# A hybrid decoder layer on one NeuronCore: preparing two RWKV head pairs together, and taking x from a transposed copy

## The chip, the cores and the metric

The kernel runs on one core of a Trainium2 chip. A core has TensorE (PE in the profile; its weight loads are PEld), VectorE (DVE), ScalarE (ACT), GpSimd (POOL) and SyncE (SP), which only issues transfers here. Matmul results go to PSUM, everything else lies in SBUF. The metric is the device time in microseconds of one execution, the median of several runs.

## The reference: what is computed

One layer over 2048 tokens of width 1024, in float32. With h = RMSNorm(x), one projection p = h @ w_in gives the inputs of three branches, their gates, and three merge gates:

```
y_a = rwkv7_mix(p_r, p_k, p_v, p_w, p_a, ...) * silu(z_a)        # 8 heads of 64, delta rule
y_b = sliding_window_sink_attn(p_q, p_sk, p_sv, ...) * silu(z_b)  # window 128
y_c = memory_cross_attn(p_xq, mem, ...) * silu(z_c)               # 256 memory tokens
merged = sum over i of sigmoid(gate_i) * (y_i @ w_proj_i)
out = x + merged @ w_out
```

The part that the change touches most is the RWKV branch. Per head, with a state S, it computes at each token

```
kk = k * k_k / max(norm(k * k_k), 1e-12)        # norm over the 64 channels of a head
k  = k * (1 + (a - 1) * k_a)
S  = S * w + (S @ -kk) (kk * a)^T + v k^T ;  y = S @ r
bonus = sum(r * k * r_k) * v                     # sum over the 64 channels
```

and then normalizes y per head and adds the bonus.

## The kernel before, in words

The tokens are worked in four blocks of 512 (`TB`). For block 0 the weights come from their inputs, are split into a high and a low part (L403 and L404) and kept in DRAM; the later blocks load the split form. A float32 product is made of three matmuls of the dense kind (L421 to L423 in `gemm3`; L1077 to L1079 in the output): high by high, high by low, low by high. Other products and all transposes run on plain float32 operands.

h is kept channels by tokens. `x_norm` loads 128x512 pieces of x with tokens on rows, squares and sums them, scales the rows (L450), and transposes them on TensorE (L455), and L459 and L460 split the result into `hH` and `hL`.

In a block two streams are woven: `stream_r`, the RWKV branch, and `stream_f`, the cross-attention heads, the sliding-window heads, the merges of those two branches and the gates of the third. After both follow the merge of the RWKV branch, `x_norm` for the next block, and `output`.

`stream_r` takes the eight heads as four pairs (128 rows hold two heads) and two pairs as a group. For each pair `rwkv_prep` projects k, computes decay and rates, and takes the key norm: squares, a matmul with `bones` that sums over a head's channels (L471, tokens on rows), a reciprocal, and `bcast_T`, which spreads the eight columns over channels (L480) and transposes them back (L482) so that L675 can scale by them. Gram matrices of the 8 chunks of 64 tokens follow (L701, masked at L706 and L707), and then the inverse of a unit triangular matrix per chunk: within 32x32 blocks by substitution on VectorE, 31 steps of a shuffle and two tensor operations (L720 to L722), and between blocks by 32x32 products on TensorE (L743, L761). The bonus is one full-precision matmul of r·k with `rep`, which holds r_k (L748, L749). `rwkv_chain` then runs the chunks of the group in turn: L798 and L799, L806, L791 and L813 on TensorE, with L801, L809, L810 and L814 on VectorE between them.

The first pair's QE, QO, AB and BK have tiles of their own; those of a group's second pair take four of the eight weight buffers (`whl`). PSUM tiles `mm`, `rw` and `as_` have two buffers each, and `rt`, the temporaries, six.

The order on each engine is made by a planner. `weave` and the numbers that the generators yield, times `PACE`, set in which order the program is written. `lay_out` then places the instructions by costs and by rank (the place in the written program; weight loads are moved ahead, the substitution behind), and `order` ties each engine to that order.

## Time and profile before

| | us |
|---|---|
| median of 3 runs | 2376.18 (2374.49 to 2379.42) |
| the profiled execution | 2371.67 |
| its span, first to last instruction | 2369.9 |
| TensorE busy in the span | 2300.5 |
| VectorE busy | 1543.7 |
| ScalarE busy | 886.2 |
| GpSimd busy | 121.6 |

The profile is of one execution, and shares and sums refer to its span. A row of a group gives line, engine, operation, output and input tiles, shapes and count, then the busy time and the mean length in ns of one, then the engine's idle time just before such instructions and what ended it. A row of a timeline gives start and length in us. Matmuls overlap, so what one costs in a stream is the distance between starts, not its length. PEclk is the granted TensorE clock as a share of full.

### The profile page before, as it was taken

Reading aid. Unit: us, or ns where it says so; the run is one execution under the profiler, and the core shown is the slowest. Engines: PE = TensorE matmul, PEld = TensorE weight load, DVE = VectorE, ACT = ScalarE, POOL = GpSimd, SP = SyncE. Lnnn points to the kernel's source line nnn. Section 1 sums busy time; section 2 is a strip of 40 time slices with the busy share of each in tenths; the row PEclk is TensorE's granted clock in tenths of the full one; section 3 lists DMA queues with packets and bytes.
Section 4 is the critical chain, followed back from the end, with each engine's and each line's share of the span. In section 5 each row is a group of like instructions: output and inputs, shape, how many; then the busy total and the mean of one; then the engine's idle time right before and its main releaser. Section 6 shows DMA issues by size and latency. Waiting matters only on the chain. (4 is left out here: it accounts for less than half of the span.)

```text
span 2369.9 us, 38481 instructions
## 1 busy us (share of the span) xinstructions
PE 2300.5 (97%) x14048; PEld 1851.8 (78%) x14048; DVE 1543.7 (65%) x4830; ACT 886.2 (37%) x1973; POOL 121.6 (5%) x183
## 2 busy tenths in 40 slices
PE   7998799999999999999999999999999999999999
PEld 6876577778887777878888877777888877877887
DVE  7988688863668868952238867784144895886312
ACT  6454535453324344332113434443122434344110
POOL 1000100000000000000000001000000000000000
PEclk9999889999999999999999999999999999999999
DMA  7755526578844443446573433435566344243655
GB/s 243 258 195 199 187 84 224 200 264 322 310 152 145 153 150 109 143 146 218 194 260 121 150 125 126 151 125 206 194 208 223 119 153 151 95 146 116 209 192 194
DMA packets 142780, 424.36 MB, mean 179 GB/s; under 512 B 16256, under 2 KB 20736, under 8 KB 142592
## 3 DMA queue, kind: packets, MB, share of 16 engines
q1 hardware_dynamic: 129920, 398.83, 48.8%
q10 hardware_dynamic: 12672, 23.07, 2.9%
q8 instruction: 112, 1.84, 0.3%
q14 instruction: 76, 0.62, 0.1%
HBM read 326.95 MB, written 94.90 MB: 178 GB/s over the span
## 5 line engine op out<-in xcount | busy, mean ns | idle before, releaser
L421 PE MATMUL mm<-hH,whl 128*128 128x512 f32 x1888 | 759.3, 402 | 6.5 <-ACT g L1044 4.4
L422 PE MATMUL mm<-hL,whl 128*128 128x512 f32 x1888 | 750.3, 397 | 0.0
L423 PE MATMUL mm<-hH,whl 128*128 128x512 f32 x1888 | 750.0, 397 | 0.0
L421 PEld LDWEIGHTS mm<-hH,whl 128*128 128x128 f32 x1888 | 357.5, 189 | 80.4 <-ACT g L1044 6.2
L423 PEld LDWEIGHTS mm<-hH,whl 128*128 128x128 f32 x1888 | 356.8, 189 | 72.4 <-issue 1.2
L422 PEld LDWEIGHTS mm<-hL,whl 128*128 128x128 f32 x1888 | 357.5, 189 | 71.0 <-issue 2.2
L1059 DVE SCALAR_TENSOR_TENSOR g<-g,mm 128x512 f32<-128x512 f32 x64 | 43.7, 683 | 223.3 <-PE mm L423 223.3
L403 ACT ACTIVATE whl<-raw 128x512 fp32r<-128x512 f32 x178 | 111.2, 628 | 186.9 <-PE mm L423 111.3
L404 DVE TENSOR_TENSOR whl<-raw,whl 128x512 fp32r<-128x512 f32 x178 | 121.6, 687 | 64.1 <-ACT whl L403 62.6
L1044 ACT ACTIVATE g<-mm 128x512 f32<-128x512 f32 x96 | 57.0, 594 | 276.5 <-PE mm L423 276.1
L421 PE MATMUL mm<-yh,whl 128*128 128x512 f32 x384 | 151.9, 396 | 0.0
L422 PE MATMUL mm<-yl,whl 128*128 128x512 f32 x384 | 150.8, 393 | 0.0
L423 PE MATMUL mm<-yh,whl 128*128 128x512 f32 x384 | 150.5, 392 | 0.0
L721 DVE TENSOR_TENSOR ibc<-ibc,Yi 128x248 f32<-128x248 f32 (+30 forms) x496 | 143.4, 289 | 10.7
L720 DVE STREAM_SHUFFLE ibc<-Nc 128x248 f32<-128x248 f32 (+30 forms) x496 | 149.4, 311 | 0.0
L722 DVE TENSOR_TENSOR Yi<-Yi,ibc 128x248 f32<-128x248 f32 (+30 forms) x496 | 140.9, 284 | 2.1
L804 ACT ACTIVATE SP<-Z,Pl 64x64 f32<-64x64 f32 x256 | 88.4, 345 | 142.0 <-DVE Z L814 138.4
L1013 ACT ACTIVATE g<-g,mxs,st 128x256 f32<-128x256 f32 (+1 forms) x128 | 74.4, 583 | 53.3 <-DVE mxs L1006 53.3
L814 DVE SCALAR_TENSOR_TENSOR Z<-rw,Pl,SP 64x64 f32<-64x64 f32 x224 | 63.4, 283 | 44.8 <-PE rw L813 41.2
L421 PEld LDWEIGHTS mm<-yh,whl 128*128 128x128 f32 x384 | 72.1, 188 | 15.6 <-issue 0.2
L422 PEld LDWEIGHTS mm<-yl,whl 128*128 128x128 f32 x384 | 72.1, 188 | 14.8 <-issue 0.2
L423 PEld LDWEIGHTS mm<-yh,whl 128*128 128x128 f32 x384 | 72.1, 188 | 14.7
(1790 smaller groups left out, 3690.1 us busy)
## 6 DMA issues: line engine op xcount, KB each, us to landing
whl<-k SPq DMA_DIRECT2D x486, 512.0 KB, 3.3
k<-whl SPq DMA_DIRECT2D x162, 512.0 KB, 3.0
raw<-in_w_in SPq DMA_DIRECT2D x118, 256.0 KB, 3.6
g<-in_x ACTq DMA_DIRECT2D x32, 256.0 KB, 5.7
out<-g ACTq DMA_DIRECT2D x32, 256.0 KB, 4.5
raw<-in_w_proj SPq DMA_DIRECT2D x24, 256.0 KB, 3.3
rt<-in_x ACTq DMA_DIRECT2D x24, 256.0 KB, 5.4
km<-mk SPq DMA_DIRECT2D x16, 256.0 KB, 2.7
```

Of the source, the lines that this page charges most:

```text
L403: S.activation(w[:, 0], raw, AF.Copy)
L404: V.tensor_tensor(w[:, 1], raw, w[:, 0].bitcast(F32), op=ALU.subtract)
L421: PE.matmul(out, lh, rh, start=i == 0, stop=False)
L422: PE.matmul(out, lh, rl, start=False, stop=False)
L423: PE.matmul(out, ll, rh, start=False, stop=i == n - 1)
L720: V.stream_shuffle(bc[:, :, :n], Nc[:, :, s + 1:], [s] * 32)
L721: V.tensor_tensor(bc[:, :, :n], bc[:, :, :n], Y[:, :, s:s + 1].to_broadcast([128, NC_, n]), op=ALU.mult)
L722: V.tensor_tensor(Y[:, :, s + 1:], Y[:, :, s + 1:], bc[:, :, :n], op=ALU.add)
L804: S.activation(SP[h, i], Z[h, i, e, c], AF.Copy, scale=g[4][h, c:c + 1])
L814: upds = [V.scalar_tensor_tensor(Sst[h, g[0]] if c == NC_ - 1 else Z[h, i, e, c + 1], pS[h, i, e], g[4][h, c:c + 1], SP[h, i], op0=ALU.mul ...
L1013: S.activation(prs[b][:, i, m0:], prs[b][:, i, m0:], AF.Exp, scale=r2[:, b, i:i + 1], bias=mx[:, b, i:i + 1], accum_out=mx[:, b, 2 + i:3 + i])
L1044: S.activation(t, gp, AF.Tanh, scale=0.5)
```

## The change

- `rwkv_prep` no longer spreads the key norm over channels. The reciprocals stay with tokens on rows in a tile `dk`. They enter in two places: GpSimd writes the mask times `dk` into AB ahead of the Gram matrices (L664 and L665 of the new file), and L700 multiplies by that; in the chain the copies of the solved rows become products with `dk` (L813).
- The bonus is computed with `hr_k` multiplied into r·k on VectorE, a split of that into a high and a low part, and two dense matmuls with a matrix of ones (L719, L720).
- The inverse moves out of `rwkv_prep` into `rwkv_inverse`, once per group: the substitution runs over the 16 chunks of both pairs (L743 to L745 in the new file), and the 32x32 products (L758, L764) follow for both.
- For blocks 1 to 3, x is also read from a transposed input. `x_scales` loads the token rows, takes the row scales and spreads them over rows by one `bcast_T`; it stands ahead of the RWKV branch's merge. `x_cols` loads channel rows, scales and splits them; it stands where `x_norm` stood. Block 0 keeps `norm_T`.
- `PACE` of the second stream goes from 1.531 to 1.42, and the yields in the preparation change.

```diff
-PACE = [[[1.0] * 120, [1.531] * 120] for _ in range(2)]
+PACE = [[[1.0] * 120, [1.42] * 120] for _ in range(2)]
...
+    ones2 = bp.tile([128, 128], F32R, name="ones2")
+    S.activation(ones2.rearrange("p (a b) -> p a b", a=2), bones.unsqueeze(2).to_broadcast([128, 2, 64]), AF.Copy)
...
-    def rwkv_prep(p, i, Z, sb, hT, lwla, group):
+    def rwkv_prep(p, i, Z, dk, Nc, sb, hT, lwla, group):
...
-        rs = xp.tile([128, 8], F32, name="st8", bufs=2)
-        V.tensor_scalar(rs, st[:, :8], 1e-24, None, op0=ALU.max)
-        V.reciprocal(rs, rs)
-        rs2 = rw_ps()
-        bcast_T(rs2, rs, 2, 4)
+        sums, own = st[:, :8].rearrange("p (a e) -> p a e", e=2), dk[:, i].rearrange("p (a o) -> p a o", o=2)
+        for e, h in ((0, EV), (1, OD)):
+            for o, at in ((0, EV), (1, OD)):
+                V.tensor_scalar(own[h, :, o], sums[at, :, e], 1e-24, None, op0=ALU.max)
+        V.reciprocal(dk[:, i], dk[:, i])
+        G.tensor_copy(AB[:, :, C:], gmask[:, C:].unsqueeze(1).to_broadcast([128, NC_, C]))
+        G.tensor_tensor(AB[:, :, :C], gmask[:, :C].unsqueeze(1).to_broadcast([128, NC_, C]), dk[:, i].unsqueeze(2).to_broadcast([128, NC_, C]), op=ALU.mult)
         kkh = tmp()
         V.tensor_scalar(kkh, k, dcol("hk_k", p), None, op0=ALU.mult)
-        t1 = tmp()
-        V.tensor_tensor(chunks(t1), chunks(kkh), Pt[:, :, :C], op=ALU.mult)
         for Q, h in ((QE, EV), (QO, OD)):
-            V.scalar_tensor_tensor(Q[h, :, :C], chunks(t1)[h], -2.0, chunks(rs2)[h], op0=ALU.mult, op1=ALU.mult)
+            V.scalar_tensor_tensor(Q[h, :, :C], chunks(kkh)[h], -2.0, Pt[h, :, :C], op0=ALU.mult, op1=ALU.mult)
...
-        V.tensor_tensor(r, r, k, op=ALU.mult)
+        V.scalar_tensor_tensor(r, r, dcol("hr_k", p), k, op0=ALU.mult, op1=ALU.mult)
...
-                V.tensor_tensor(AB[h, c0:c0 + 4], g[h], gmask[h].unsqueeze(1).to_broadcast([64, 4, 128]), op=ALU.mult)
+                V.tensor_tensor(AB[h, c0:c0 + 4], g[h], AB[h, c0:c0 + 4], op=ALU.mult)
...
-        rkb = xp.tile([128, 2, 64], F32, name="rep", bufs=2)
-        V.tensor_scalar(rkb, bones.unsqueeze(2).to_broadcast([128, 2, 64]), dcol("hr_k", p), None, op0=ALU.mult)
-        PE.matmul(pb, rkb.rearrange("p a b -> p (a b)"), r, start=True, stop=True)
+        rkh, rkl = (rp.tile([128, TB], F32R, name="rt", bufs=NRT) for _ in range(2))
+        S.activation(rkh, r, AF.Copy)
+        V.tensor_tensor(rkl, r, rkh.bitcast(F32), op=ALU.subtract)
+        PE.matmul(pb, ones2, rkh, start=True, stop=False)
+        PE.matmul(pb, ones2, rkl, start=False, stop=True)
...
+    def rwkv_inverse(group, Z, Nc):
+
+        n = len(group) * NC_
...
+        for s in range(31):
+            w = 31 - s
+            bc = rp.tile([128, n, 32], F32, name="ibc", bufs=2)
+            V.stream_shuffle(bc[:, :, :w], N_[:, :, s + 1:], [s] * 32)
+            V.tensor_tensor(bc[:, :, :w], bc[:, :, :w], Y[:, :, s:s + 1].to_broadcast([128, n, w]), op=ALU.mult)
+            V.tensor_tensor(Y[:, :, s + 1:], Y[:, :, s + 1:], bc[:, :, :w], op=ALU.add)
+        yield 27
...
-            V.tensor_copy(Z[EV, :n, 0, c], pu[EV])
-            upd = V.tensor_copy(Z[OD, :n, 1, c], pu[OD])
+            for e, h in ((0, EV), (1, OD)):
+                upd = V.tensor_tensor(Z[h, :n, e, c], pu[h], dk[h, :n, c:c + 1].to_broadcast([64, n, C]), op=ALU.mult)
...
+    def x_cols(sb, rb):
+
+        hi, lo = hT_tiles()
+        for k in range(8):
+            xt = tmp()
+            nc.scalar.dma_start(xt, A["xt"][k * 128:(k + 1) * 128, sb * TB:(sb + 1) * TB])
+            V.tensor_tensor(xt, xt, rb, op=ALU.mult)
+            g = pcol("norm_g", k)
+            S.activation(hi[:, k], xt, AF.Copy, scale=g)
+            V.scalar_tensor_tensor(lo[:, k], xt, g, hi[:, k].bitcast(F32), op0=ALU.mult, op1=ALU.subtract)
+        return hi, lo
...
+                yield from rwkv_inverse(group, Z, Nc)
...
+        rb = x_scales(sb + 1) if sb + 1 < nsb else None
         for _ in merge(0, *ya, accs, hT, gates=gates):
             pass
-        if sb + 1 < nsb:
-            hT = x_norm(sb + 1)
+        if rb is not None:
+            hT = x_cols(sb + 1, rb)
         output(sb, accs)
```

Three places show how the planned order moves. The names: `mm`, `rw` and `as_` are PSUM tiles, `c_ident` the identity matrix (so the row is a transpose), `yh`/`yl` and `hH`/`hL` split operands, `whl` a weight buffer.

TensorE before, from the merge of block 0 into its output:

```order
L422 MATMUL mm<-yl,whl 128x512
L423 MATMUL mm<-yh,whl 128x512
L455 MATMUL rw<-c_ident,rt 128x128 x8
L1077 MATMUL mm<-whl,g_6493 128x512
L1078 MATMUL mm<-whl,g_6493 128x512
L1079 MATMUL mm<-whl,mB 128x512
```

TensorE now, at the start of that merge, where the only transposes for x stand:

```order
L423 MATMUL mm<-hH,whl 128x512
L476 MATMUL as__5964<-c_ident,rt 128x128 x4
L421 MATMUL mm<-yh,whl 128x512
L422 MATMUL mm<-yl,whl 128x512
L423 MATMUL mm<-yh,whl 128x512
```

Of the 32 transposes among the output's matmuls none is left; four stand ahead of the merge.

TensorE before, at the inverse of the second pair of the first group in block 2 (`ibc` and `Yi` are the substitution's tiles, `rep` holds r_k):

```order
L743 MATMUL rw<-ibc,whl 32x32 x16
L749 MATMUL rw<-rr__13190,rep 128x512
L421 MATMUL mm<-hH,whl 128x512
L422 MATMUL mm<-hL,whl 128x512
L423 MATMUL mm<-hH,whl 128x512
L421 MATMUL mm<-hH,whl 128x512
L422 MATMUL mm<-hL,whl 128x512
L754 MATMUL rw<-c_ident,rk__13587 128x128 x4
L761 MATMUL rw<-Yi,ibc 32x32 x16
```

TensorE now, at the joint inverse of the same group:

```order
L758 MATMUL rw<-ibc,AB 32x32 x16
L758 MATMUL rw<-ibc,whl 32x32 x16
L1000 MATMUL as__13444<-KsH,g_13294 128x256
L1000 MATMUL as__13444<-KsL,g_13294 128x256
L1000 MATMUL as__13444<-KsH,g_13294 128x256
L1000 MATMUL as__13444<-KsL,g_13294 128x256
L422 MATMUL mm<-hL,whl 128x512
L423 MATMUL mm<-hH,whl 128x512
L421 MATMUL mm<-hH,whl 128x512
L764 MATMUL rw<-Yi,ibc 32x32
L422 MATMUL mm<-hL,whl 128x512
L423 MATMUL mm<-hH,whl 128x512
```

Both pairs' 32x32 products now stand together with attention scores (L1000) and projections between them. The bonus (L719, L720) and the transposes of v (L725) have moved ahead of the substitution; from the second pair's last transpose of v to the first row shown there are 190 rows of other TensorE work.

VectorE before, at the start of the substitution of the first pair of the first group in block 1 (`g_7165` and `yl` belong to the other stream):

```order
L707 TENSOR_TENSOR QE<-rw,gmask 64x512
L867 TENSOR_TENSOR yl<-g_7165,yh 128x512
L720 STREAM_SHUFFLE ibc<-Nc 128x8x31
L720 STREAM_SHUFFLE ibc<-Nc 128x8x30
L721 TENSOR_TENSOR ibc<-ibc,Yi 128x8x31
L722 TENSOR_TENSOR Yi<-Yi,ibc 128x8x31
```

VectorE now, at the start of the joint substitution of that group:

```order
L701 TENSOR_TENSOR whl<-rw,gmask 64x512 x2
L901 SCALAR_TENSOR_TENSOR mx<-mx,st_7269 128x4
L743 STREAM_SHUFFLE ibc<-Nc 128x16x31
L743 STREAM_SHUFFLE ibc<-Nc 128x16x30
L744 TENSOR_TENSOR ibc<-ibc,Yi 128x16x31
L745 TENSOR_TENSOR Yi<-Yi,ibc 128x16x31
```

The same three operations run over 16 chunks instead of 8, once, behind the Gram matrices of both pairs instead of behind each pair's.

On GpSimd each pair adds a cast (L664) and a mask product (L665) of 512 elements per row, among the two-step powers that the norms of both streams take there.

More of the change, by code (lines that the diff above doesn't have):

```diff
@@ L758, in rwkv_prep @@
             S.activation(Zc[EV, 1, :, o], pv_[h, :, 1], AF.Copy)
-        for c in range(NC_):
+        group.append((p, (QE, QO), AB, BK, Pl, yt))
+        yield 2.5
+    def rwkv_inverse(group, Z, Nc):
+        n = len(group) * NC_
+        halves = [(slice(b, b + 32), slice(b + 32, b + 64)) for b in (0, 64)]
+        N_ = Nc.rearrange("p i c t -> p (i c) t")
+        Y = rp.tile([128, n, 32], F32, name="Yi")
+        V.tensor_copy(Y, eye32.unsqueeze(1).to_broadcast([128, n, 32]))
+        for s in range(31):
[5 more added lines that the diff above has]
+        yield 27
+        X = rp.tile([128, n, 32], F32, name="ibc", bufs=2)
+        V.transpose(X.rearrange("p a b -> p (a b)"), Y.rearrange("p a b -> p (a b)"))
+        for i, g in enumerate(group):
+            for q in range(4):
+                qs = slice(32 * q, 32 * q + 32)
+                S.activation(g[2][qs, :, 32 * (q % 2):32 * (q % 2) + 32], Y[qs, i * NC_:(i + 1) * NC_], AF.Copy)
+        R = rp.tile([128, n, 32], F32, name="ibc", bufs=2)
+        pr = rw_ps().rearrange("p (c t) -> p c t", t=32)
+        for i, g in enumerate(group):
+            for c in range(NC_):
+                for u, l in halves:
+                    PE.matmul(pr[l, i * NC_ + c], g[2][u, c, 32:64], X[u, i * NC_ + c], start=True, stop=True)
+        for u, l in halves:
+            V.tensor_copy(R[l], pr[l])
+        po = rw_ps().rearrange("p (c t) -> p c t", t=32)
+        for c in range(n):
@@ L772, in rwkv_chain @@
+        yield 4
+        for i, g in enumerate(group):
+            for e, h in ((0, EV), (1, OD)):
+                S.activation(Z[h, i, e, 0], Sst[h, g[0]], AF.Copy)
+    def rwkv_chain(group, Z, dk, hT, yas):
         n = len(group)
@@ L1199, in host @@
     A["x"] = g["x"][0]
+    A["xt"] = g["x"][0].T
     A["mem"] = g["mem"][0]
```

84 lines of the change are left out of this document (34 added, 50 removed).

## The prediction

> **What bounds the kernel now.** I read the busy times of the page first, then the stages, then what TensorE waited for, then its instructions in time.
>
> ```profile
> span 2369.9 us, 38481 instructions
> PE 2300.5 (97%) x14048; PEld 1851.8 (78%) x14048; DVE 1543.7 (65%) x4830; ACT 886.2 (37%) x1973; POOL 121.6 (5%) x183
> ```
>
> ```profile
> core 0: us, PE busy (x) PEld busy (x) DVE busy (x) ACT busy (x) POOL busy (x), PEclk, DMA share, GB/s
> 60.00:330.00 270.00, 241.38 (x1494) 191.12 (x1494) 218.85 (x642) 126.90 (x271) 19.26 (x27) 0.91 0.55 189
> 330.00:659.30 329.30, 326.01 (x1903) 261.73 (x1902) 228.11 (x659) 149.90 (x323) 9.95 (x14) 1.00 0.71 252
> 659.30:1230.20 570.90, 563.43 (x3474) 454.03 (x3473) 354.96 (x1150) 195.01 (x444) 28.66 (x41) 1.00 0.48 164
> 1230.20:1799.80 569.60, 563.17 (x3473) 454.17 (x3472) 354.82 (x1150) 195.06 (x444) 27.80 (x41) 1.00 0.48 164
> 1799.80:2369.90 570.10, 559.46 (x3441) 450.91 (x3439) 344.77 (x1122) 182.82 (x412) 24.97 (x34) 1.00 0.45 155
> ```
>
> The cuts are the ends of the output projections, so the last three rows are token blocks 1, 2 and 3 (the last with its final transfer). TensorE is busy for 563 of 570 us there, at the full clock, and VectorE for 355, 62%. These blocks are as long as TensorE's work, and a microsecond of that work taken away is a microsecond of time as long as the other engines keep delivering. Block 0 is different: between 60 and 330 us TensorE stands for 28.6 us, the clock is 0.91 of full, which is another 270 x 0.09 = 24 us of missing pulses (partly under the standing time), and VectorE is busy for 219 of 270 us, 81%, because there the weights are also split. The waits say the same: the long ones come once each.
>
> ```profile
> PE rw L455 <- DVE g L450: 9.9, 1, 9.9
> PE as__2849 L997 <- DVE g L979: 7.7, 1, 7.7
> PE rw L842 <- DVE rt L839: 7.2, 5, 6.2
> ```
>
> **The change, part by part.**
>
> *Transposes.* Blocks 1 to 3 lose 32 transposes of x each (96), the 16 head-pair preparations lose the four that spread the key norm over channels (64), and three blocks gain the four that spread the row scales of x (12): 148 fewer. What one costs is read where eight stand between dense matmuls:
>
> ```profile
> 1182.11 0.40 PE L423 MATMUL mm<-yh,whl 128*128 128x512 f32 x1
> 1182.34 1.04 PE L455 MATMUL rw<-c_ident,rt 128*128 128x128 f32 x8
> 1183.13 0.47 PE L1077 MATMUL mm<-whl,g 128*128 128x512 f32 x1
> 1183.45 0.39 PE L1078 MATMUL mm<-whl,g 128*128 128x512 f32 x1
> ...
> L455 PE MATMUL rw<-c_ident,rt 128*128 128x128 f32 x104 | 15.2, 275 | 1.8 <-DVE mB L460 1.4 <-DVE rt L450 0.4
> L482 PE MATMUL rw<-c_ident,rt 128*128 128x128 f32 x64 | 9.6, 272 | 0.0
> ```
>
> Dense matmuls start 0.23 us apart (1182.11 to 1182.34). From 1182.34 to 1183.45 eight transposes and one dense matmul go by: 1.11 - 0.23 = 0.88, so 0.110 us each. 148 x 0.110 = 16.3 us. The wait of 0.4 us for L450 goes with them; nothing in that stage stands behind it but dense matmuls.
>
> The Trainium skill, "TensorE: Matmul & The Clock Gate", Part 4 (PE-mode transpose), gives about 275 ns for a transpose in one kernel's context; an estimate by that page would be 148 x 0.275 = 40.7 us. The mean durations in the rows agree with the page, 275 and 272 ns, but the start times do not agree with using it as a price: the instructions overlap.
>
> *The bonus matmul.* Before, one full-precision matmul of 128x512, recorded as two; after, two split ones of the dense kind.
>
> ```profile
> 1384.04 1.13 PE L749 MATMUL rw<-rr__13190,rep 128*128 128x512 f32 x2
> 1384.61 0.80 PE L421 MATMUL mm<-hH,whl 128*128 128x512 f32 x1
> 1385.24 0.40 PE L422 MATMUL mm<-hL,whl 128*128 128x512 f32 x1
> ```
>
> From 1384.04 to 1385.24 it and one dense matmul pass: 1.20 - 0.23 = 0.97 us. The new form is two dense starts, 0.46. 16 x 0.51 = 8.2 us. Everything else on TensorE has the same count: statistics, Gram matrices, the 32x32 products of the inverse, the chain. TensorE's sum is **-24.5 us**.
>
> *Joint substitution.* It stays on VectorE: 31 steps of three instructions, now 16 chunks wide instead of 8, once for two pairs.
>
> ```profile
> L721 DVE TENSOR_TENSOR ibc<-ibc,Yi 128x248 f32<-128x248 f32 (+30 forms) x496 | 143.4, 289 | 10.7
> L720 DVE STREAM_SHUFFLE ibc<-Nc 128x248 f32<-128x248 f32 (+30 forms) x496 | 149.4, 311 | 0.0
> L722 DVE TENSOR_TENSOR Yi<-Yi,ibc 128x248 f32<-128x248 f32 (+30 forms) x496 | 140.9, 284 | 2.1
> ...
> L720 DVE STREAM_SHUFFLE ibc<-Nc 128x248 f32<-128x248 f32 x16 | 7.0, 438 | 0.0
> L722 DVE TENSOR_TENSOR Yi<-Yi,ibc 128x248 f32<-128x248 f32 x16 | 6.6, 414 | 0.4
> L721 DVE TENSOR_TENSOR ibc<-ibc,Yi 128x248 f32<-128x248 f32 x16 | 6.4, 398 | 0.0
> ```
>
> Before: (143.4 + 149.4 + 140.9) / 16 = 27.1 us a pair, 54.2 a group. After, the mean width is 256 elements, nearest to the 248 of the last three rows: 31 x 1.25 = 38.8, say 39.6 us with the eight elements more. VectorE is relieved of 14.6 us a group, 117 us in all, and a group's inverse is ready 39.6 instead of 27.1 us after its second pair's Gram matrices, 12.5 us later. In blocks 1 to 3 neither counts while TensorE has other work. In block 0's stretch up to 330 us VectorE is what is waited for. One group's substitution falls in there, and the gain lies between 0 (the waits stay) and 14.6 us (VectorE bound throughout). Since TensorE is busy for 241 of the 270 us and VectorE for 219, I take a value nearer the lower end, **-4 us**.
>
> *Small VectorE, ScalarE and POOL edits.* Rows for what goes and for the nearest of what comes:
>
> ```profile
> L673 DVE TENSOR_TENSOR rt<-rt,Pt 128x512 f32<-128x512 f32 x16 | 11.0, 688 | 0.3
> L480 DVE COPY rt<-st 128x512 f32<-128x512 f32 x20 | 8.5, 426 | 1.8 <-POOL st L390 1.3
> L810 DVE COPY Z<-rw 64x128 f32<-64x128 f32 x64 | 18.9, 295 | 1.9
> L826 DVE TENSOR_TENSOR rt<-yps,st 128x256 f32<-128x256 f32 x32 | 12.6, 418 | 0.5
> L1091 POOL CAST amask<-g 128x256 bf16<-128x256 f32 x1 | 0.6, 591 | 0.0
> L390 POOL TENSOR_TENSOR var<-var,mhalf 128x8 f32<-128x8 f32 x16 | 27.5, 1716 | 1.3
> ```
>
> A pair loses one product (L673, 0.69) and one spreading copy (L480, 0.43) and gains one subtraction of the split (0.69) and a few 4-element operations: about even. ScalarE gains one 512-wide copy a pair and is 37% busy. In the chain the copy at L809 and L810 becomes a product with a scale, at least 0.295 and at most the twice as wide 0.418, so at most 0.12 x 2 later at each of the eight steps, 2 us a group. A POOL cast of 512 elements costs about 2 x 0.59 = 1.2 us and its product with two inputs 1.2 to 2.4; behind them on POOL stand the powers of the other branches' norms (1.7 us each), which VectorE and then TensorE wait for. All of this I put at nothing in blocks 1 to 3. Its cover is the projections, gates and merges of the other stream. In block 2's first group 190 rows of TensorE now stand between the second pair's last transposes and the first 32x32 product. If that cover fails, the cost is the first rival.
>
> *x by columns.* Per block VectorE does eight products and eight split steps of 512 elements (0.69 each, as L673) where it did eight scalings and sixteen split steps of 256:
>
> ```profile
> L450 DVE TENSOR_SCALAR rt<-rt,rs 128x512 f32<-128x512 f32 x28 | 12.1, 483 | 5.1 <-POOL rs L390 5.0
> L460 DVE SCALAR_TENSOR_TENSOR hL<-rw,c_pv,hH 128x256 fp32r<-128x256 f32 x56 | 25.6, 479 | 10.6 <-ACT hH L459 10.0
> 1162.00:1230.20 68.20, 67.77 (x315) 55.89 (x314) 29.25 (x52) 13.24 (x28) 0.89 (x2) 1.00 0.71 238
> ```
>
> That is 11.0 us against 8 x 0.483 + 16 x 0.479 = 11.5: equal. The new h can be written only after the block's last gate projection and is needed by the next block's first one; the last row is the merge and the output of block 1, which lie between. VectorE has 39 us free there. Eight more loads of 256 KB a block, 2.1 MB, are 9 us at this row's 238 GB/s, and the DMA engines have 29% of 68 us free. It costs nothing; if it came late, the next block's first projection would wait.
>
> *Sum.* 2371.7 (the profiled execution) - 24.5 - 4 = 2343. The median of the runs is 4.5 us above that execution, so **2348 us**.
>
> **Rivals.**
>
> 1. *TensorE runs dry at the joint inverse (slower).* The 32x32 products and the whole chain now hang on one 39.6 us substitution, and the pace of the other stream was changed too. If TensorE stands through half of the 12.5 us by which the inverse is later, 8 x 6.3 = 50 us: 2398. It decides from 28.5 / 8 = 3.6 us of standing a group. Against it: the substitution of a group's second pair already took 45 us from its first to its last row in block 2, with other work between its steps, and TensorE waited for the product behind it for 0.9 us in the whole run.
>
> ```profile
> 1335.98 0.42 DVE L722 TENSOR_TENSOR Yi<-Yi,ibc 128x248 f32<-128x248 f32 x1
> 1381.27 0.18 DVE L722 TENSOR_TENSOR Yi<-Yi,ibc 128x8 f32<-128x8 f32 x1
> PE rw L743 <- DVE ibc L725: 0.9, 1, 0.9
> ```
>
> Chance 0.10.
>
> 2. *Block 0 clears up.* With VectorE lighter, the single waits of 7.7 and 6.2 us and the half-clock windows beside them go: 13.9 us of waiting and a quarter of the 24 us of clock, 20 us more, 2328. For it: those waits name VectorE. Against: the relief is 14.6 us and other chains wait too. Chance 0.15.
>
> 3. *Block 0 gets worse.* The new order puts a wait of that kind at another place, as long as the two longest there together, 14 us: 2362. For it: those waits are chains that came late by chance of the order, and the whole order and the other stream's pace are new. Against it: VectorE has less to do. Chance 0.17.
>
> 4. *POOL holds VectorE up.* Each pair's new POOL work, 2.4 to 3.6 us, delays VectorE in full; felt where VectorE is the bound, four pairs of block 0: 14 us, 2362. The Trainium skill, "SBUF — State Buffer", Who interferes with whom, has such a rule: a VectorE instruction with two SBUF inputs and a POOL instruction that reads SBUF exclude each other. No row here shows POOL beside VectorE long enough to tell. Chance 0.06.
>
> 5. *No change beyond what can be measured.* The gain is eaten by many small waits of a microsecond, as there is one at the transposes of L1028 now in each block, of which these are the first and the last.
>
> ```profile
> PE as__3059 L1028 <- DVE g L1024: 1.9, 1, 1.9
> PE as__19852 L1028 <- DVE g L1024: 1.8, 1, 1.8
> ```
>
> It would take 24 us of them, some 13 new ones of that size. Chance 0.05.
>
> **How the numbers follow.** The forecast as worked out, 2337 to 2360, has 0.47; its bounds are the 14.6 us for block 0 and the chain's 2 us a group on the other side. Faster by over 0.2% (4.8 us, about what a measurement of this kernel can tell) are it and rivals 2, 3 and 4: 0.85; same 0.05; slower 0.10. The range takes in rivals 2, 3 and 4 and leaves out most of the first: 2326 to 2372.
>
> **What would show it.** In the changed profile: blocks 1 to 3 about 6 us shorter each with TensorE still standing for under 10 us (right), or a wait of the 32x32 product for the substitution of several microseconds in each group (rival 1). No transposes of x between the output's matmuls. VectorE's busy time near 1425 us. Between 60 and 330 us the clock and the standing time tell rivals 2 and 3 apart. VectorE's 512-wide instructions with two SBUF inputs longer than 0.69 us beside POOL's would be rival 4. The forecast is wrong if block lengths stay at 570 us although the counts have fallen.

## The result, and the profile after

The changed kernel takes 2344.0 us (median of 4 runs, 2341.75 to 2348.01) against 2375.3 (median of 4, 2371.3 to 2379.4): a ratio of 0.9874, with a 95% interval of 0.9857 to 0.9890. The forecast was 2348, the range 2326 to 2372. The profiled execution took 2344.03 us. Of the runs further down, one execution of c_key, at a mean clock of 0.64, took 3251.8 us; its median and its ratio leave that one out.

The page of the changed kernel, its first lines:

```profile
span 2342.1 us, 37181 instructions
PE 2272.2 (97%) x13900; PEld 1834.3 (78%) x13900; DVE 1475.0 (63%) x3798; ACT 894.6 (38%) x1969; POOL 149.3 (6%) x209
```

The same stages as in the prediction, cut again at the ends of the output projections, with the same columns:

```profile
60.00:330.00 270.00, 246.21 (x1569) 195.96 (x1568) 219.29 (x547) 138.94 (x301) 25.39 (x35) 0.94 0.56 196
330.00:644.80 314.80, 309.04 (x1790) 248.32 (x1789) 211.69 (x492) 140.69 (x292) 12.85 (x12) 0.99 0.76 267
644.80:1210.00 565.20, 557.48 (x3429) 450.70 (x3428) 337.38 (x890) 196.94 (x441) 34.31 (x47) 0.99 0.49 169
1210.00:1774.50 564.50, 556.71 (x3430) 450.12 (x3429) 337.27 (x890) 196.67 (x441) 34.26 (x47) 0.99 0.49 170
1774.50:2342.10 567.60, 556.55 (x3424) 450.21 (x3423) 327.80 (x872) 185.74 (x416) 31.01 (x41) 0.99 0.45 155
```

Block 0 ends 14.5 us earlier (644.8 against 659.3). Blocks 1 and 2 are 5.7 and 5.1 us shorter, block 3 is 2.5 us shorter. TensorE is busy for 6.0, 6.5 and 2.9 us less in them, so these blocks are still nearly as long as TensorE's work. The clock in blocks 1 to 3, which was 1.00, is now 0.99. The waits of TensorE say why:

```profile
PE rw L447 <- DVE g L442: 10.5, 1, 10.5
PE as__2611 L1000 <- DVE g L982: 10.1, 1, 10.1
PE rw L695 <- DVE QO L683: 6.5, 1, 6.5
PE as__8314 L1000 <- DVE g L982: 4.7, 1, 4.7
PE as__13428 L1000 <- DVE g L982: 4.7, 1, 4.7
PE as__18542 L1000 <- DVE g L982: 4.7, 1, 4.7
PE mm L1082 <- DVE mB L1071: 3.7, 1, 3.7
```

There is a wait of 4.7 us in each of blocks 1 to 3 that was not there before: the attention scores (L1000) stand until the query is split (L982). In time, TensorE's rows around that wait in block 1:

```profile
788.11 0.39 PE L423 MATMUL mm<-yh,whl 128*128 128x512 f32 x1
788.34 0.95 PE L463 MATMUL as__8302<-c_bones,g 128*128 128x2 f32 x8
794.00 0.55 PE L1000 MATMUL as__8314<-KsH,g 128*128 128x256 f32 x1 [4.72 <-DVE g L982]
...
796.90 0.63 PE L421 MATMUL mm<-hH,whl 128*128 128x512 f32 x1
797.33 0.63 PE L422 MATMUL mm<-hL,whl 128*128 128x512 f32 x1
...
801.08 0.69 PE L758 MATMUL rw<-ibc,AB 32*32 32x32 f32 x32
801.61 0.67 PE L758 MATMUL rw<-ibc,whl 32*32 32x32 f32 x32
```

Ahead of the wait dense matmuls start 0.23 us apart (788.11 to 788.34 is one), behind it 0.43 (796.90 to 797.33): the clock record has half the clock until 799.7. So a wait costs more than its own length, here 4.7 us of standing and half of the 5.4 us that TensorE is busy from 794.0 to 799.7, 2.7 us. The last two rows are the joint inverse's 32x32 products, 0.5 us for each 32, with no wait ahead of them. (The Trainium skill, "TensorE: Matmul & The Clock Gate", Part 1, gives 426.7 and 215.7 ns between 512-column starts at half and at full clock, and about 3.4 us without work as what halves it. The trace agrees, with 0.43 and 0.23 us behind and ahead of a wait of 4.72.)

What VectorE does meanwhile, some of its rows in the same stretch:

```profile
775.12 0.68 DVE L509 SCALAR_TENSOR_TENSOR g<-g,g 128x512 f32<-128x512 f32 x1
775.72 0.35 DVE L745 TENSOR_TENSOR Yi<-Yi,ibc 128x192 f32<-128x192 f32 x1
...
785.87 2.77 DVE L961 TENSOR_TENSOR KsL<-g,KsH 64x512 fp32r<-64x512 f32 x4
...
793.17 0.68 DVE L982 TENSOR_TENSOR g<-g,g 64x512 fp32r<-64x512 f32 x1
```

It is busy for 19.1 of the 19.2 us from 774.0 to 793.2: rotary tables (L506 to L515), the keys' rotation (L521 to L524), the split of the keys (L961), and between them the steps of the joint substitution (L743 to L745). The query comes last. The second row starts before the first has ended (775.12 + 0.68 = 775.80): VectorE's instructions overlap by some hundredths of a microsecond.

The groups that answer to those of the sum:

```profile
L743 DVE STREAM_SHUFFLE ibc<-Nc 128x496 f32<-128x496 f32 (+30 forms) x248 | 113.3, 472 | 0.1
L744 DVE TENSOR_TENSOR ibc<-ibc,Yi 128x496 f32<-128x496 f32 (+30 forms) x248 | 104.3, 421 | 3.5
L745 DVE TENSOR_TENSOR Yi<-Yi,ibc 128x496 f32<-128x496 f32 (+30 forms) x248 | 103.1, 416 | 1.1
L813 DVE TENSOR_TENSOR Z<-rw,dk 64x128 f32<-64x128 f32 x128 | 36.9, 288 | 49.2 <-PE rw L809 35.0 <-ACT SP L807 5.2 <-PE yps L802 3.3
```

The substitution takes 320.7 us in all, where the three groups of before took 433.7: 113 us less, 117 were worked out. The chain's product with `dk` is no dearer (288 ns) than the copies it replaced (295). GpSimd's casts and products take 30.8 us in all, 1.9 a pair, where 2.4 to 3.6 were allowed.

### The profile page after: what moved, and what is told of

It reads as the page before. It is cut to its first block, busy times and chain, and to the rows that moved or that the text cites. A ratio compares the mean times of both kernels' runs of the same rounds, so it can differ in the third digit from the quotient of the medians.

```text
span 2342.1 us, 37181 instructions
## 1 busy us (share of the span) xinstructions
PE 2272.2 (97%) x13900; PEld 1834.3 (78%) x13900; DVE 1475.0 (63%) x3798; ACT 894.6 (38%) x1969; POOL 149.3 (6%) x209
## 4 chain that ended last, share of the span: by engine, by line
PE 68%; DVE 17%; ACT 2%; issue 1%; POOL 1%; DMA 0%; DVEq 0%; ACTq 0%; POOLq 0%
PE mm L421 16%; PE mm L422 16%; PE mm L423 16%; DVE ibc L743 3%; DVE Yi L745 2%; DVE ibc L744 2%; PE rw L695 1%; PE mm L1082 1%; PE mm L1080 1%; PE mm L1081 1%; PE oo L1036 1%; PE rw L816 1%; PE rw L809 1%; PE rw L801 1%; POOL var L390 1%
## 5 line engine op out<-in xcount | busy, mean ns | idle before, releaser
L421 PE MATMUL mm<-hH,whl 128*128 128x512 f32 x1888 | 758.6, 402 | 3.1 <-ACT g L1047 3.1
L423 PE MATMUL mm<-hH,whl 128*128 128x512 f32 x1888 | 750.6, 398 | 0.0
L421 PEld LDWEIGHTS mm<-hH,whl 128*128 128x128 f32 x1888 | 357.2, 189 | 76.8 <-ACT g L1047 4.5
L423 PEld LDWEIGHTS mm<-hH,whl 128*128 128x128 f32 x1888 | 357.3, 189 | 73.7 <-issue 1.4
L404 DVE TENSOR_TENSOR whl<-raw,whl 128x512 fp32r<-128x512 f32 x178 | 123.3, 696 | 78.7 <-ACT whl L403 77.7
L421 PE MATMUL mm<-yh,whl 128*128 128x512 f32 x384 | 151.5, 395 | 0.1
L423 PE MATMUL mm<-yh,whl 128*128 128x512 f32 x384 | 151.5, 394 | 0.0
L743 DVE STREAM_SHUFFLE ibc<-Nc 128x496 f32<-128x496 f32 (+30 forms) x248 | 113.3, 472 | 0.1
L744 DVE TENSOR_TENSOR ibc<-ibc,Yi 128x496 f32<-128x496 f32 (+30 forms) x248 | 104.3, 421 | 3.5
L745 DVE TENSOR_TENSOR Yi<-Yi,ibc 128x496 f32<-128x496 f32 (+30 forms) x248 | 103.1, 416 | 1.1
L1087 DVE SCALAR_TENSOR_TENSOR g<-mm,g 128x512 f32<-128x512 f32 x16 | 11.0, 690 | 116.8 <-PE mm L1082 116.8
L421 PEld LDWEIGHTS mm<-yh,whl 128*128 128x128 f32 x384 | 72.1, 188 | 15.3 <-DVE g L1062 0.9
L423 PEld LDWEIGHTS mm<-yh,whl 128*128 128x128 f32 x384 | 72.1, 188 | 14.7
```

The lines of the kernel that those rows point to most:

```text
L404: V.tensor_tensor(w[:, 1], raw, w[:, 0].bitcast(F32), op=ALU.subtract)
L421: PE.matmul(out, lh, rh, start=i == 0, stop=False)
L423: PE.matmul(out, ll, rh, start=False, stop=i == n - 1)
L743: V.stream_shuffle(bc[:, :, :w], N_[:, :, s + 1:], [s] * 32)
L744: V.tensor_tensor(bc[:, :, :w], bc[:, :, :w], Y[:, :, s:s + 1].to_broadcast([128, n, w]), op=ALU.mult)
L745: V.tensor_tensor(Y[:, :, s + 1:], Y[:, :, s + 1:], bc[:, :, :w], op=ALU.add)
```

## The experiments

For each kernel three numbers were worked out from its profiled execution. *Standing* is the span less TensorE's busy time. *Clock loss* is half of the time that TensorE was busy at the halved clock, from the trace's clock records. *Work* is what is left of the span: TensorE's work at full clock. For the changed kernel: 2342.1 - 2272.2 = 69.9 standing, 17.6 clock loss, 2254.6 work. For the kernel before: 69.4, 22.9 and 2277.6.

| kernel | median us | ratio to before (95%) | span | standing | clock loss | work | block 0 ends |
|---|---|---|---|---|---|---|---|
| before | 2375.3 | | 2369.9 | 69.4 | 22.9 | 2277.6 | 659.5 |
| changed | 2344.0 | 0.9874 (0.9857 to 0.9890) | 2342.1 | 69.9 | 17.6 | 2254.6 | 644.8 |
| u_x | 2346.7 | 0.9893 (0.9877 to 0.9908) | 2342.7 | 65.8 | 14.5 | 2262.4 | 641.2 |
| u_bonus | 2349.1 | 0.9904 (0.9888 to 0.9920) | 2346.4 | 69.6 | 18.1 | 2258.7 | 646.3 |
| u_key | 2334.4 | 0.9843 (0.9827 to 0.9858) | 2332.1 | 58.7 | 13.5 | 2259.9 | 634.8 |
| u_split | 2368.1 | 0.9979 (0.9969 to 0.9989) | 2362.0 | 74.5 | 34.5 | 2253.0 | 652.0 |
| a_pace | 2363.4 | 0.9946 (0.9932 to 0.9961) | 2360.6 | 76.0 | 22.6 | 2262.1 | 647.4 |
| b_pace | 2354.4 | 0.9905 (0.9890 to 0.9920) | 2352.9 | 54.4 | 14.2 | 2284.3 | 650.2 |
| b_rope | 2334.4 | 0.9836 (0.9814 to 0.9857) | 2334.2 | 40.9 | 11.0 | 2282.2 | 640.2 |
| a_rope | 2314.9 | 0.9736 (0.9720 to 0.9752) | 2314.7 | 52.6 | 9.5 | 2252.6 | 641.3 |
| c_key | 2314.4 | 0.9754 (0.9735 to 0.9772) | 2312.6 | 40.7 | 8.9 | 2263.0 | 632.7 |
| c_pace | 2316.8 | 0.9762 (0.9743 to 0.9780) | 2315.2 | 40.1 | 12.0 | 2263.2 | 634.4 |
| h_key | 2308.8 | 0.9731 (0.9716 to 0.9745) | 2306.6 | 41.7 | 6.3 | 2258.6 | 632.5 |
| h_both | 2304.8 | 0.9721 (0.9704 to 0.9737) | 2302.8 | 40.1 | 2.6 | 2260.0 | 629.1 |

*Work* is as exact as the records of TensorE's busy time and clock that it is reckoned from. The ratios are to the kernel before on the same chip; its medians there lay between 2372.4 and 2376.0 us. Where a difference between two kernels is given as two numbers, these are by the medians and by the ratios (times 2375); the second has an interval of some 5 us to either side.

The theory to test was that of the prediction: the gain is TensorE work taken away, and VectorE's relief matters a little, in block 0. The rival: it is mostly the new order of the instructions, of which the other stream's pace is a part, and the parts by themselves are worth less than their work.

### One part undone at a time

These four ran on one chip. *u_x* takes x by transposes again in all blocks:

```diff
-        rb = x_scales(sb + 1) if sb + 1 < nsb else None
...
-        if rb is not None:
-            hT = x_cols(sb + 1, rb)
+        if sb + 1 < nsb:
+            hT = x_norm(sb + 1)
```

> The new kernel with the x of blocks 1 to 3 again from 32 transposes each. Theory A (the gain is TensorE's work, term by term): 84 more transposes at 0.110 us, +9.2 us on 2344, so 2353, with TensorE's busy time up by 9.2 us. Theory B (the gain is the new order's, which relieves block 0): TensorE's busy time goes up as well but the span stays within 4 us of 2344, and block 0 keeps its 644 us end whatever the transposes do.

Measured: 2346.7 us, 2.7 above the changed kernel by the medians and 4.5 by the ratios. TensorE's work rises by 7.8 us, close to the 84 x 0.110 = 9.2 us of the 84 transposes that come back. But standing and clock loss fall by 7.2 us, 6.0 of them in block 0, which ends 3.6 us earlier although its work has grown. So x by columns takes the work away nearly as reckoned, and does not come at nothing. In the changed kernel, the last wait of 3.7 us listed above (L1082 for L1071) lies where the new rows stand on VectorE among the weight splits of block 0:

```profile
600.54 1.41 DVE L1128 SCALAR_TENSOR_TENSOR hL<-rt,c_pv,hH 128x512 fp32r<-128x512 f32 x2
601.87 0.68 DVE L404 TENSOR_TENSOR whl<-raw,whl 128x512 fp32r<-128x512 f32 x1
...
603.13 2.86 DVE L1071 TENSOR_TENSOR mB<-mB,g 128x512 fp32r<-128x512 f32 x4
```

The output of block 0 waits for L1071, which is queued behind them.

*u_bonus* puts the full-precision bonus matmul back:

```diff
-        PE.matmul(pb, ones2, rkh, start=True, stop=False)
-        PE.matmul(pb, ones2, rkl, start=False, stop=True)
+        rkb = xp.tile([128, 2, 64], F32, name="rep", bufs=2)
+        V.tensor_scalar(rkb, bones.unsqueeze(2).to_broadcast([128, 2, 64]), dcol("hr_k", p), None, op0=ALU.mult)
+        PE.matmul(pb, rkb.rearrange("p a b -> p (a b)"), r, start=True, stop=True)
```

> The new kernel with the bonus as one full-precision matmul per pair again. Theory A: 16 x 0.51 = +8.2 us, 2352. Theory B: within 4 us of 2344.

Measured: 2349.1 us, 5.1 to 7.1 more. Work rises by 4.1 us, standing and clock loss by 0.2. In this trace the full-precision matmul takes 0.86 us from its start to the next instruction's (in the eight pairs where transposes follow), the split pair 0.46: 0.40 a pair, 6.4 us in all, where the prediction had 0.51 and 8.2. The prediction read its price behind the 32x32 products. About half of the predicted amount came back as work.

*u_key* takes the key norm over channels again, with its transposes. AB is masked by the plain mask, the chain copies, and the new GpSimd work is gone:

```diff
-        G.tensor_tensor(AB[:, :, :C], gmask[:, :C]..., dk[:, i]..., op=ALU.mult)
...
+        rs2 = rw_ps()
+        bcast_T(rs2, rs, 2, 4)
...
-                upd = V.tensor_tensor(Z[h, :n, e, c], pu[h], dk[h, :n, c:c + 1].to_broadcast([64, n, C]), op=ALU.mult)
+            V.tensor_copy(Z[EV, :n, 0, c], pu[EV])
+            upd = V.tensor_copy(Z[OD, :n, 1, c], pu[OD])
```

> The new kernel with the key norm spread over channels by transposes again; GpSimd's mask products and the chain's scale products go. Theory A: 64 x 0.110 = +7.0 us, 2351. If GpSimd's products delayed VectorE (the fourth rival of the prediction), taking them out gives some of it back: 2340 to 2347. Theory B: within 4 us of 2344.

Measured: 2334.4 us, 7.4 to 9.6 *less* than the changed kernel, although TensorE has 5.3 us more to do. Standing and clock loss fall by 15.3 us, and block 0 ends 10.0 us earlier. The place is the wait of 6.5 us at L695. First the changed kernel there, then u_key, in the same stretches:

```profile
294.00:298.00 4.00, 1.25 (x11) 1.08 (x9) 3.88 (x10) 0.00 (x0) 1.66 (x4) 1.00 0.17 65
298.00:302.00 4.00, 0.24 (x2) 0.28 (x4) 3.93 (x6) 0.00 (x0) 3.13 (x2) 0.50 0.00 0
302.00:306.00 4.00, 2.27 (x17) 1.98 (x18) 3.63 (x7) 2.37 (x4) 0.00 (x0) 0.50 0.00 0
```

```profile
294.00:298.00 4.00, 3.93 (x29) 3.26 (x28) 3.94 (x13) 0.98 (x2) 1.82 (x3) 1.00 0.10 36
298.00:302.00 4.00, 4.00 (x22) 3.36 (x21) 3.96 (x14) 0.01 (x1) 0.67 (x2) 1.00 0.02 4
302.00:306.00 4.00, 4.00 (x19) 3.33 (x18) 3.94 (x9) 1.12 (x2) 0.00 (x0) 1.00 0.00 0
```

VectorE is full in both. In the changed kernel TensorE has nothing to do in between and falls to half clock; in u_key it has. TensorE's rows from the sum ahead of the wait to the Gram matrices (L695), again the changed kernel first:

```profile
294.30 0.95 PE L463 MATMUL as__3212<-c_bones,g 128*128 128x2 f32 x8
301.75 0.55 PE L695 MATMUL rw<-QO,BK 64*128 64x128 f32 x1 [6.50 <-DVE QO L683]
```

```profile
294.09 0.95 PE L463 MATMUL as__3225<-c_bones,g 128*128 128x2 f32 x8
294.89 0.31 PE L1000 MATMUL as__3237<-KsH,g 128*128 128x128 f32 x1
...
306.94 0.39 PE L422 MATMUL mm<-hL,whl 128*128 128x512 f32 x1
307.26 0.37 PE L695 MATMUL rw<-QO,BK 64*128 64x128 f32 x1
```

The new rows do not make the Gram matrices' operand late. VectorE's last row for it (L683, writing QO) ends 10 us behind the sums of the key norm in the changed kernel (291.46 to 301.61 us) and 15 us behind them in u_key (291.70 to 307.07). But in u_key attention scores and projections stand in between on TensorE, and in the changed kernel nothing does behind 294.30. So this wait, too, is one of the planned order, which the part brought with it.

*u_split* runs the substitution once per pair, as before, with all else as changed (and the yields of before behind it):

```diff
                     yield from rwkv_prep(p, p - p0, Z, dk, Nc, sb, hT, lwla, group)
-                yield from rwkv_inverse(group, Z, Nc)
+                    yield from rwkv_inverse(group[-1:], Z, Nc[:, p - p0:p - p0 + 1], p - p0)
```

> The new kernel with the substitution per pair again, everything else new. TensorE's work is the same. Theory A with VectorE's relief: 117 us of VectorE's time come back (busy near 1590), block 0 loses what it gained beyond TensorE's work (8 us), and the new 4.7 us wait of the scores in blocks 1 to 3, which stands in the middle of the joint substitution, goes (3 x 4): between 2340 and 2352. Theory B: the joint substitution is the gain, and the time goes back to 2365 or more.

Measured: 2368.1 us, 24 to 25 more. TensorE's work is the same within 1.6 us; what is added is standing (4.6 us) and, above all, clock loss (16.9 us). VectorE's busy time is 1553.1 us, 78 more. The waits of 4.7 and 6.5 us are gone, but others have grown; four of the eight longest sums of TensorE's waits:

```profile
PE rw L801 <- DVE Z L817: 11.6, 11, 1.4
...
PE rw L816 <- DVE Z L813: 8.2, 12, 0.9
PE rw L809 <- DVE W L804: 4.4, 7, 1.1
...
PE rw L758 <- DVE ibc L748: 3.4, 1, 3.4
```

The first three are the chain's steps, which now wait for VectorE. But VectorE is not full there. The chain of block 0's first group, in u_split and then in the changed kernel:

```profile
233.70:281.90 48.20, 35.40 (x351) 27.56 (x350) 24.02 (x81) 19.91 (x56) 1.92 (x3) 0.62 0.06 20
```

```profile
228.50:275.40 46.90, 46.45 (x442) 33.98 (x437) 30.77 (x91) 26.56 (x68) 1.91 (x2) 1.00 0.47 163
```

VectorE is busy for half of that time in u_split and for two thirds of it in the changed kernel. What u_split lacks is cover: 20 dense matmuls (L421 to L423) stand among the chain's steps, and 105 in the changed kernel. In blocks 1 to 3 the first chain has 57 of them against 85, and the second 219 against 109. So u_split shows that the substitution per pair, with the yields of before and the new pace, gives an order in which the first chains stand bare. It costs time in every block (blocks 1 to 3 take 568 to 570 us), but the 21.5 us are no price of VectorE's relief, which this run does not isolate.

### The pace, and where the rotary tables stand

*a_pace* is the changed kernel with the old pace, *b_pace* the kernel before with the new one:

```diff
-PACE = [[[1.0] * 120, [1.42] * 120] for _ in range(2)]
+PACE = [[[1.0] * 120, [1.531] * 120] for _ in range(2)]
```

> The new kernel with the old pace of the second stream, 1.531 instead of 1.42. TensorE's work is the same to a microsecond. If the waits of block 0 and the 4.7 us waits follow from where the order puts things, they move: 2335 to 2360, with the difference in standing time and half clock alone. If VectorE's relief is what shortened block 0, block 0 still ends within 5 us of 644.

> The kernel before with the new pace, 1.42. TensorE's work stays that of the kernel before. If the pace alone cleared block 0, it gains the 8 us that block 0 gained beyond TensorE's work: 2367. If the pace does nothing or was set for the new program, 2370 to 2385.

Measured: 2363.4 us for a_pace, 17 to 19 more than the changed kernel, and 2354.4 for b_pace, 22 less than the kernel before. At the old pace the whole rest of the change is worth 12.6 us (2376.0 to 2363.4), at the new one 7 to 10. A single number moves more than all the parts together. It does not show in TensorE's instructions: b_pace has the same 14048 matmuls as the kernel before. What falls is standing and clock loss (92.3 to 68.6), while work itself rises by 6.7 us. In a_pace the work is 7.5 us above the changed kernel's with the same instructions. So the order alone changes TensorE's work by some 7 us, and no single term of the sum can be checked more finely than that by undoing it.

In the changed kernel the rotary tables are computed just ahead of the sliding-window keys, which puts them in the stretch before the 4.7 us wait. *a_rope* and *b_rope* compute them at the start of the other stream; b_rope is the kernel before with that and with the new pace:

```diff
         def stream_f():
+            rope_tables(sb)
             for h in range(4):
...
-            rope_tables(sb)
             yield from swa_kv(sb, hT)
```

> The new kernel with the rotary tables of a block computed at the start of its second stream instead of ahead of the keys, where their 20 VectorE operations of 512 elements now stand among the joint substitution. If that crowding is what makes the scores wait 4.7 us in each of blocks 1 to 3, the wait and the half clock behind it shrink: 3 x (4.7 + 1.7) = up to 19 us less, 2325 to 2340. If the wait has another cause (VectorE in its fixed order standing for a gate's activation), it stays near 4.7 us and the time within 4 us of 2344.

> The kernel before with the new pace (1.42) and the rotary tables at the start of the second stream, the two edits of order that cost no TensorE work, to compare with the new kernel that has the same two (2314.9). Theory A (TensorE's work is what the change itself is worth): the difference between the two is the difference of their TensorE work, 23 to 32 us, so 2338 to 2347. Theory B (the change is worth nothing beyond its order): with the same pace and the same place of the tables the two are within 6 us, 2309 to 2321.

Measured: 2314.9 us for a_rope, 29 to 33 less than the changed kernel, which is more than the 19 us expected at most; 2334.4 for b_rope, 16 to 20 less than b_pace. The longest waits of a_rope behind that of the start:

```profile
PE rw L695 <- DVE QO L683: 7.0, 2, 6.5
PE mm L1082 <- DVE mB L1071: 3.7, 1, 3.7
PE as__2611 L1000 <- DVE g L982: 3.6, 1, 3.6
```

The three waits of 4.7 us are gone, the one of 10.1 us is 3.6 us, and blocks 1 to 3 take 557.4, 556.2 and 556.1 us, 8 us less each. The same stretch of block 1, from the changed kernel and then from a_rope:

```profile
780.00:812.00 32.00, 27.02 (x264) 21.39 (x263) 24.04 (x89) 14.16 (x29) 0.00 (x0) 0.89 0.26 93
```

```profile
780.00:812.00 32.00, 31.88 (x371) 24.80 (x369) 20.13 (x73) 11.54 (x29) 0.00 (x0) 1.00 0.31 101
```

This shows that the wait came from the order on VectorE: the tables are needed late, and early there is room for them.

Between b_rope and a_rope, pace and tables stand alike, and what is left is the change itself. It is worth 19.5 us by the medians and 24 by the ratios (give or take 6): 29.6 us of work less, but 10.2 us more of standing and clock loss (51.9 to 62.1). In blocks 1 to 3 the work taken away comes back in full: they are 7.2, 8.7 and 4.8 us shorter, for 6.8, 7.7 and 4.4 us of work less. In block 0 it does not: up to its end standing and clock loss grow by 11.7 us (38.6 to 50.3), and it ends at the same time in both (640.2 and 641.3 us). So the theory holds in blocks 1 to 3 and fails in block 0.

The rival holds for the gain as it was measured: of some 31 us the pace alone makes 17 to 22, and at the new pace the parts, with 29.7 us of work less (2284.3 to 2254.6), are worth 7 to 10. It does not hold once the tables stand early. Whether the joint substitution, or the old pace, would do the same with the tables early was not run.

### Where a part pays and where it doesn't

If the key norm on token rows costs time in block 0 and saves TensorE work in the others, then it should be taken block by block. *c_key* is a_rope with u_key's edit in all blocks, *c_pace* is c_key at a pace of 1.36, *h_key* is a_rope with u_key's edit in block 0 alone, and *h_both* is h_key with x for block 1, which is prepared in block 0, by transposes:

```diff
+        if sb:
+            V.reciprocal(dk[:, i], dk[:, i])
...
+        else:
+            rs2 = rw_ps()
+            bcast_T(rs2, rs, 2, 4)
...
-        rb = x_scales(sb + 1) if sb + 1 < nsb else None
+        rb = x_scales(sb + 1) if 0 < sb < nsb - 1 else None
...
             hT = x_cols(sb + 1, rb)
+        elif not sb:
+            hT = x_norm(1)
```

> The new kernel with the tables early and the key norm again spread over channels by transposes. If the 9.6 us that this undoing gained without the early tables is a wait that GpSimd's mask products and the small operations on dk cause in block 0 (6.5 us of standing and the half clock behind it), it gains again what is left of that, 7 to 10 us less its 5 to 7 us of TensorE work came out positive before: 2303 to 2310. If it was an accident of one order, the transposes cost their 5 to 7 us: 2320 to 2322.

> As the last, with pace 1.36 in place of 1.42. TensorE's work within 7 us (between the two paces tried on the new kernel it was 7.5 us), the rest waits: 2300 to 2325, no side expected.

> The new kernel with the tables early and the key norm spread over channels in block 0 only. If the scales on token rows pay in blocks 1 to 3 (TensorE's work, about 2 us a block) and cost only where VectorE is full (block 0, 8.6 us between the kernels with and without them), both gains add: 2315.6 - 3 x 2.2 = 2309, with block 0 ending near 633 us. If their cost in block 0 was one unlucky order, block 0 ends near 641 us again: 2315.

> As the last, and x of block 1 from transposes again, since the columns of x for block 1 are prepared in block 0, where VectorE still splits weights and TensorE stood 3.7 us behind them. If that wait and the half clock behind it (1.7 us) are worth more than 28 transposes (3.1 us): 2 us less than the last, 2307. If the transposes cost their full price and the wait stays: 2312.

Measured: c_key 2314.4 us, the same as a_rope by the medians and 4 us more by the ratios. It lies between the two cases that were expected: block 0 is 8.6 us shorter than a_rope's, blocks 1 to 3 are 1.5 to 2.7 us longer, work is 10.4 us more, standing and clock loss are 12.5 us less. c_pace at 2316.8 is 2.4 us slower by the medians, with intervals of the ratios that overlap: between 1.36 and 1.42 the pace makes no clear difference here.

h_key took 2308.8 us, as expected (2309), and h_both 2304.8, 2 us less than expected. The longest waits of h_both:

```profile
PE rw L455 <- DVE g L450: 10.0, 1, 10.0
PE as__2620 L1022 <- DVE g L1004: 5.1, 1, 5.1
```

Its block 0 ends at 629.1 us, 15.7 us earlier than the changed kernel's, with 2.6 us of clock loss left in the whole run. Its ratio, 0.9721, is well below the changed kernel's 0.9874: h_both is faster than both kernels. Whether it is faster than a_rope is not settled: their ratios (0.9721 and 0.9736) have intervals that overlap, since the kernel before ran 3.6 us faster on the chip of h_key and h_both. What the traces show of the mechanism does not depend on that: block 0 of h_key is 8.8 us shorter than a_rope's, and blocks 1 to 3 together are as long (1674.1 and 1673.4 us).

## Why the prediction was right

The total (2348 against 2344.0) and its direction were right, and so was the main term, TensorE's work. That the total came so near is in part luck, since waits that the sum didn't have took and gave some 20 us each. Between the two profiled executions the time fell by 27.6 us (2371.67 to 2344.03), and the sum had 28.5; the 4.5 us by which the median of before lay above its profiled execution have no counterpart in the changed kernel. Point by point:

- *Transposes and bonus, -24.5 us of TensorE.* TensorE's work fell by 23.0 us. Undone one by one, x returns 7.8 of 9.2 us, the key norm 5.3 of 7.0 and the bonus 4.1 of 8.2; together 17.2; the other 5.8 lie within what the order alone moved elsewhere (6.7 and 7.5 us), and were not traced to a part. The bonus was mis-sized: its price was read from one place, behind 32x32 products, and is 0.40 us a pair instead of 0.51 elsewhere.
- *Blocks 1 to 3 about 6 us shorter each, under 10 us standing.* Blocks 1 and 2: 5.7 and 5.1 us, with 7.7 and 7.8 us standing. Block 3: 2.5 us, with 11.0 us standing (10.6 before, the final transfer among it). The forecast of 6 for block 3 overlooked that it prepares no x; its own part of the sum is 16 x 0.110 + 4 x 0.51 = 3.8 us. The part of the sum of blocks 1 and 2 is 6.9 each; the half clock behind the new wait takes some of it back.
- *Block 0's relief, -4 us.* Standing and clock loss fell by 4.8 us in all (92.3 to 87.5): by 8.9 up to the end of block 0, and they grew by 4.1 behind it. The size is right by luck, since it is a sum of other terms. The pace, which the prediction named without a price, takes 23.7 us of them away (92.3 to 68.6 in b_pace), and the parts put 18.9 back at that pace (68.6 to 87.5). Undone one at a time, the key norm gives back 15.3 us of them and x by columns 7.2, and both were put at nothing. What the joint substitution's relief is worth was not isolated. The nearest comparison is b_rope with h_both, which in block 0 have the same pace, tables, key norm and way to take x: up to the end of block 0 standing and clock loss are 38.6 and 31.2 us, 7.4 less with the joint substitution and the split bonus. That lies between the 0 and 14.6 us of the prediction. In blocks 1 to 3, where it allowed for nothing, b_rope and a_rope differ by 1.6 us (13.3 and 11.7).
- *"It costs nothing" for x by columns, and "at nothing" for the small edits.* In blocks 1 to 3 this holds as far as the waits named there go: the chain's product is no dearer, no wait for GpSimd's new work shows, and no gate projection waits for x. In block 0 it failed in two ways: the rows for x hold up the output on a full VectorE (3.7 us at L1082), and the Gram matrices of the key norm's part follow their sums on TensorE with nothing to cover VectorE's 10 us in between (6.5 us at L695).
- *VectorE's busy time near 1425 us.* It is 1475.0, 69 us less than before instead of 119. The durations behaved as reckoned: summed over all instructions they fell from 1766.6 to 1645.7 us, by 121. But they overlap. Before, the sum is 223 us above the busy time over 4830 instructions, 46 ns each; after, 171 us over 3798, 45 ns each. Of 1032 instructions less, some 50 us of duration had never been VectorE's time. The step took durations for prices, which is what the prediction itself had warned of at the transposes. So the relief of a group, 93 instructions fewer and 14.1 us of duration (113 / 8), is by an estimate from these means nearer 10 us (14.1 - 93 x 0.046) than 14.6.
- *Rival 1, TensorE dry at the joint inverse.* Refuted. From its first to its last step a joint substitution takes 51 to 79 us, longer than the 45 us of before, and TensorE does not wait for the product behind it (rows at 801.08 above): there is other work. In u_split, with the shorter substitutions, it does wait there once, 3.4 us.
- *Rivals 2 and 3, block 0 better or worse.* Between: the waits of 7.7 and 6.2 us are gone, new ones of 10.1 and 6.5 have come, and the clock there rose from 0.91 to 0.94. Block 0 lost 14.5 us, of which 8.9 are standing and clock loss.
- *Rival 4, GpSimd holding VectorE up.* The mechanism is there, the size is not. On VectorE, the same operation beside and without a GpSimd product, and that product, at L665:

```profile
296.92 0.63 DVE L673 TENSOR_TENSOR BK<-rt 64x512 f32<-64x512 f32 x1
...
298.17 1.44 DVE L673 TENSOR_TENSOR BK<-rt 64x512 f32<-64x512 f32 x1
...
297.74 1.31 POOL L665 TENSOR_TENSOR AB<-gmask,dk 128x512 f32<-128x512 bf16 x1
```

VectorE's second instruction ends 0.8 us later than it would. Over the run such instructions, at L404 (1.42 and 1.53 instead of 0.69), L683, L718 and L671, come to some 3 us, not 14. VectorE stands in 10 of the 30.8 us of GpSimd's new work, and rows with two inputs that begin ahead of GpSimd's instruction mostly keep their length (L870 from 123.81 took 0.69 us beside L665 from 123.97 on; L404, begun at 124.42, took 1.53). (The Trainium skill, "SBUF — State Buffer", Who interferes with whom, says that a VectorE instruction with two SBUF inputs contends with a GpSimd instruction that reads SBUF, and that the shared ports are an exclusive lock. The rows shown agree: L673 stretches by about what is left of GpSimd's, 299.05 - 298.17 = 0.88 us.)

## What to carry to other kernels

Work taken from the engine that is the bound comes back as time where no new wait eats it: in blocks 1 to 3 with the tables early 18.9 us of work gave 20.7 us, while at the order of the changed kernel 29.7 us of work gave 7 to 10. The waits that a change makes or clears by its new order can be as large as the work, of either sign, so a forecast should price the change of order (here the pace and the place of the rotary tables) and not only the parts. An engine that is busy for 62% on average is no free cover: some waits came from stretches of 10 to 20 us in which it was full. Others came where it was not full, but where little other work stood beside a chain of steps. So undoing a part tells its price only in the order that it is undone in, and the order's own waits have to be looked at in each run. A part can be kept in the stages where it pays and left out where it costs, as h_key and h_both do.

## What was not expected of the hardware

VectorE's instructions overlap, by 45 ns on average in this kernel, so many small ones cost less than the sum of their durations. A single wait of 4.7 us at the full clock takes the TensorE clock to half for some microseconds behind it: dense matmuls start 0.43 instead of 0.23 us apart until 5.7 us after work resumes. With the 6.5 us wait of block 0, which has short pauses around it, the half clock lasts for 13.6 us (298.0 to 311.6 us by the clock record). It can also come of many short waits: in u_split's first chain none behind that of 3.4 us is longer than 1.4 us, and the clock stays at half from 229.6 to 270.6 us, with TensorE busy for 27.6 of these 41.0. TensorE's work at full clock, by the reckoning of the table, varies by some 7 us between orders of the very same instructions (b_pace against before, a_pace against changed), which the profile's counts and durations don't show.
